# One stage of a chunked RWKV-7 scan is woven in two slots earlier, an addition moves from VectorE to TensorE, and three PSUM results share one bank

## The chip, the cores and the metric

The kernel runs on one core of one Trainium2 chip. The metric is the device time of one execution in microseconds. Names of engines in the profile: PE is TensorE's matrix multiplication, PEld its weight load, DVE is VectorE, ACT is ScalarE, POOL is GpSimd, SP is SyncE, which here only issues DMAs. `L12` is line 12 of the kernel that was profiled.

## The reference

A two-layer encoder over 256 positions of width 2048. Each layer normalises its input, multiplies it by one wide input projection, runs two head groups on the result, gates both, joins them and multiplies by an output projection, which is added to the residual:

```
for l in range(DEPTH):                       # DEPTH = 2
    h = rms_norm(x, norm_g[l])
    proj = h @ w_in[l]
    r, k, v, xw, xa = split(bidir_token_shift(proj[:, :3264]))
    y_rw = rwkv7_branch(r, k, v, xw, xa, ...)     # 16 heads of 64, one scan per direction
    y_at = window_attention(rope(q), rope(k_at), v_at, sink[l])
    x = x + concat([y_rw * silu(g_rw), y_at * silu(g_at)]) @ w_out[l]
return rms_norm(x, final_g)

def step(S, inp):                            # of the RWKV-7 scan, S is 64 x 64 for a head
    s_kk = S @ kk_t
    S = S * w_t - outer(s_kk, a_t * kk_t) + outer(v_t, k_t)
    return S, S @ r_t
```

The kernel replaces the 256 steps by four chunks of 64. Within a chunk the recurrence becomes a triangular system, whose inverse is built by doubling blocks and then corrected by one Newton step; the change touches that correction and the loop over chunks.

## The kernel before, in words

**The stream.** The projections are a list of steps (`Stream`, L222). A step is three matmuls on fp32r tiles (`gemm`, L273 to L275: high part of the weights by high part of the input, high by low, low by high), all 128 by 128 by 256. Eight steps use one tile of weights. It comes by DMA from SP's queue, is rounded to `hi` on ACT (L215) and has the rest put into `lo` on DVE (L216), in two halves each; two tiles have buffers.

**Windows and slots.** Everything else is woven into this stream. `layer` runs the stream 64 steps at a time (`window`, L359), and a window is cut into 14 slots. At the head of each slot some generators are advanced by one `yield`, then four or five stream steps follow. PE executes in exactly this written order (`manual_schedule`). The other engines' orders are made by the scheduler at build time, by priority, and are fixed in the program; each engine runs its own list in order. Two heads are a pair, and pair `p` goes through these generators:

- `scan_p` (L631, window `p + 1`, slots `STAGE_P`): low-rank products for decay and in-context rate (`pza`), their scans along the chunk (`lw`, L659 on DVE), the exponentials `pp` and `ip` on ACT (L662, L663), a sum over each head (`pk`, L628), reciprocal `kd` (L665 on DVE), and the operands `MV` and `BK`.
- `scan_i` (L708, window `p + 2`, every slot, and slots 0 and 1 of window `p + 3`): Gram products `pg` for direction 0 in slot 0 and for direction 1 in slot 1 (L718), both masked on DVE into `ge` (L724); a 16-bit copy `AB` on ACT (L733); in slot 2 transposes into `pt` (L741, L749), which ACT copies out as `bt` (L754) and into `suv` (L759); from slot 3 on the doubling of the inverse, with `pq` and `pd` on PE (L803, L813, L819, L821), `QF` on ACT (L815), `tv` and `tt` on DVE (L806, L822, L823). In slots 0 and 1 of the next window the Newton step: residual `pf` (L829 to L834), its copy `q16` on ACT (L836), product `pn` (L840), and `vf` = 2 `tt` + `pn` on DVE (L842).
- `scan_b` (L848, window `p + 3`, slots 1 to 13, and slot 3 of window `p + 4`): four chunk steps of three slots each. In the first slot PE multiplies the state (`pcc`, L866), ACT copies it to `rh` (L869, L872). In the second PE applies the inverse (`pu`, L885) and ACT writes the result into `suv` (L890). In the third PE updates the state (L895) and the output `py` (L902), and DVE scales the state into `suv` for the next chunk (L897). Slots 12 and 13 make the head norm (L913 to L917). The part in the next window's slot 3 is called the tail here: eight transposing matmuls (L922, 16 records in the trace), ACT's scale and bias (L924), DVE's L925 and L614, ACT's L615, DVE's L616.

So windows 1 to 8 of a layer hold a `scan_p`, 2 to 9 a `scan_i`, 3 to 10 a `scan_b`, 4 to 11 a tail. Window 3 is the one that has all of them except a tail. Windows are counted from 0; in layer 0 window 3 starts at 123.96 us of the trace, window 4 at 166.82 and window 6 at 252.54. Windows from 10 on hold attention.

**PSUM.** The scans share two rotating buffers of two banks each (`wpair`, tag `w`); a new allocation waits until the readers of the one before the last are done. `pcc` and `py` have a bank each. In a window the order of allocation is `pf`, `pg`; `pn`, `pg`; `pu`, `pt`; the tail's `pyt`, `pq`; `pq`, `pza`; and so on. So `pq` in slot 3 takes over the buffer of `pt`, which ACT empties with L754 and L759.

**Quarters of the array.** A matmul with 64 rows and 64 columns uses a quarter of PE's array: the rows are the operands' partition half, the columns the half that the result goes to. `half[h ^ d]` swaps halves for the second direction.

Of the kernel before, what the change touches and what calls it, by code (L numbers as in the profile page):

```python
# [21 lines left out]
T = 256  # L22
# [19 lines left out]


SLOTS = 14
STAGE_P = [4, 6, 7, 8, 9, 10, 11, 13]
STAGE_I = (list(range(SLOTS)), [0, 1])
STAGE_B = (list(range(1, 14)), [3])
ATT = [
    [4, 11],
    [1, 3, 6, 8, 11, 13],  # L50
# [78 lines left out]
def hybrid_trunk_kernel(ctx, tc, xT, wi, wv, wo, par, fing, dup, iup, sink, pos, cst, out):  # L129
# [21 lines left out]
    def wbank(name):  # L151
        return wpair(name)[:, 0]

    def st(tag, shape, dt=F32, bufs=1):
        return sp.tile([128, *shape], dt, tag=tag, name=tag, bufs=bufs)
# [140 lines left out]
    LV = cp.tile([128, NL, 2, 128], U8, name="LV")  # L296
    AB, AL, QF = (cp.tile([128, 2, NC, 64], F16, name=n) for n in ("AB", "AL", "QF"))
    MSK = cp.tile([128, NC, 64], F16, name="MSK")
    EYE, NEYE = (cp.tile([128, 64], F16, name=n) for n in ("EYE", "NEYE"))
    band = cp.tile([128, 512], BF16, name="band")  # L300
    FG = cp.tile([128, NKT], F32, name="FG")
    SK = cp.tile([128, DEPTH * 16], F32, name="SK")
# [3 lines left out]
    def setup():  # L306
        posi = st("t1", [T], I32, bufs=3)
        SY.dma_start(out=posi, in_=pos.to_broadcast([128, T]))
        SY.dma_start(out=FG, in_=fing)
        SY.dma_start(out=SK, in_=sink.to_broadcast([128, DEPTH * 16]))  # L310
        cin = st("mv", [C_N - C_KEEP], bufs=3)
        SY.dma_start(out=cin, in_=cst[:, C_KEEP:C_N])
        for l in range(DEPTH):
            s = DP[:, l, 0:NSH]
            V.tensor_tensor(s, PR[:, l, P_MU0 : P_MU0 + NSH], PR[:, l, P_MU1 : P_MU1 + NSH], op=ALU.add)
            V.tensor_scalar(s, s, -1.0, 1.0, op0=ALU.mult, op1=ALU.add)
            h = DP[:, l, NSH : NSH + 8]
            V.tensor_scalar(h, PR[:, l, P_KA : P_KA + 8], 0.5, None, op0=ALU.mult)
            V.tensor_scalar(DP[:, l, NSH + 8 : NSH + 16], h, -1.0, 1.0, op0=ALU.mult, op1=ALU.add)
            V.tensor_scalar(DP[:, l, NSH + 16 : NSH + 32], PR[:, l, P_A0 : P_A0 + 16], 0.5, None, op0=ALU.mult)  # L320
        V.tensor_scalar(SK, SK, 8.0, None, op0=ALU.mult)
        yield


        ang = st("g", [T], bufs=2)
        nn = st("g", [T], bufs=2)
        V.tensor_copy(ang, posi)
        V.tensor_scalar(ang, ang, C[:, C_OFF["inv"] : C_OFF["inv"] + 1], None, op0=ALU.mult)

        def reduce_by(dst, src, period, bits, shift):  # L330
            V.tensor_scalar(nn, src, 1.0 / period, shift, op0=ALU.mult, op1=ALU.add)
            V.tensor_scalar(nn, nn, MAGIC, MAGIC, op0=ALU.add, op1=ALU.subtract)
            cur = src
            for p in split_const(period, bits, 4):
                V.scalar_tensor_tensor(dst, nn, -p, cur, op0=ALU.mult, op1=ALU.add)
                cur = dst

        two_pi = 2.0 * np.pi
        reduce_by(ang, ang, two_pi * 4096.0, 7, 0.0)
        for dst, shift, add in ((SIN, 0.0, 0.0), (COS, 0.25, np.pi / 2)):  # L340
            reduce_by(dst, ang, two_pi, 11, shift)
            if add:
                V.tensor_scalar(dst, dst, float(add), None, op0=ALU.add)
            V.tensor_scalar(dst, dst, PI_IN, -PI_IN, op0=ALU.min, op1=ALU.max)
            A.activation(dst, dst, AF.Sin)
        V.tensor_scalar(SIN, SIN, C[:, C_OFF["sgn"] : C_OFF["sgn"] + 1], None, op0=ALU.mult)
        yield
        V.tensor_copy(
            LV.rearrange("p l s (n x) -> p (l s) n x", x=32),
            cin[:, 512 : 512 + 64 * NL].rearrange("p (n x) -> p n x", x=32).unsqueeze(2).to_broadcast([128, 2 * NL, NC, 32]),  # L350
        )
        V.memset(MSK, 1.0)
        V.memset(MSK[:, :, 0:1], 0.0)
        V.tensor_copy(band, cin[:, 0:512])
        V.tensor_copy(EYE, cin[:, 512 + 64 * NL : 576 + 64 * NL])
        V.tensor_scalar(NEYE, EYE, -1.0, None, op0=ALU.mult)
        yield

    def window(n, *gens, groups=SLOTS):  # L359
# [246 lines left out]
    def layer(l):  # L606
# [24 lines left out]
        def scan_p(p, t):  # L631
# [18 lines left out]
            KR = st("kkr", [T])  # L650
            A.activation(KR, K, AF.Identity, scale=prm(P_KK, p))
            yield
            pk = wbank("pk")
            head_sums(pk, sq)

            V.tensor_scalar(LW, LW, 1.0, None, op0=ALU.add)
            msk = MSK.rearrange("p c j -> p (c j)")
            for x in (LW[:, 0:T], LW[:, T : 2 * T][:, ::-1]):
                V.tensor_tensor_scan(x, msk, x, 0.0, op0=ALU.mult, op1=ALU.add)  # L659
            PP = st("pp", [2, NC, 64])  # L660
            IP = st("ip", [2, NC, 64])
            A.activation(PP.rearrange("p d c j -> p (d c j)"), LW, AF.Exp, scale=DECAY_C)  # L662
# [45 lines left out]
        def scan_i(p, t):  # L708
# [126 lines left out]
            FN = st("q16", [2, NC, 64], F16)  # L835
            A.activation(FN.rearrange("p d c j -> p d (c j)"), pf[:, :, 0:T], AF.Copy)  # L836
            yield
            pn = wbank("pn")
            for d, c, h in dch:
                PE.matmul(pn[half[h ^ d], d * T + c * 64 : d * T + (c + 1) * 64], hx(FN, d, c, h), hx(TT, d, c, h), start=True, stop=True)  # L840
            VF = st("vf", [2, NC * 64])
            V.scalar_tensor_tensor(  # L842
                VF.rearrange("p d x -> p (d x)"), TT.rearrange("p d c j -> p (d c j)"), 2.0, pn, op0=ALU.mult, op1=ALU.add
            )
            t["VF"] = VF
            yield

        def scan_b(p, t):  # L848
            GE, MV, BT, SUV, PC, bv = (t[n] for n in ("GE", "MV", "BT", "SUV", "PC", "bv"))


            pc = ps_c.tile([128, 512], F32, tag="c", name="pcc")
            pS = pc[:, 0:128].rearrange("p (d j) -> p d j", d=2)
            pyt = ps_c.tile([128, 512], F32, tag="y", name="py")
            py = pyt[:, 0:256].rearrange("p (c j) -> p c j", j=64)
            for i in range(NC):
                ci = [order[d][i] for d in range(2)]

                here = lambda h, i=i: pick(SUV, half[h], i * 128 + h * 64, [NC * 128 + (NC - 1 - 2 * i) * 128, 2], [1, 64])

                pr = [pc[:, 128:192], pc[:, 192:256] if i else pyt[:, 256:320]]
                for d in range(2):
                    for h in range(2):

                        r = half[1 - h] if i == 0 else every
                        PE.matmul(pr[d][half[h ^ d]], GE[h][r, d, ci[d], 0, :], SUV[r, d, ci[d], h, :], start=True, stop=True)  # L866
                RH = st("rh", [2, 64], bufs=2)
                if i:
                    A.activation(RH, pc[:, 128:256].rearrange("p (d j) -> p d j", d=2), AF.Copy)  # L869
                else:  # L870
                    for d in range(2):
                        A.activation(RH[:, d, :], pr[d], AF.Copy)  # L872
                yield
                if i > 0:
                    for d in range(2):
                        for h in range(2):
                            PE.matmul(
                                py[half[h], ci[d], :], MV[half[h], d, ci[d], 1, :], SUV[half[h], d, ci[d], h, :],
                                start=False, stop=False, skip_group_check=True,
                            )  # L880
                pu = wpair("pu")
                for d in range(2):
                    for h in range(2):
                        x = half[h ^ d]
                        PE.matmul(pu[half[h], d, 0:64], t["VF"][x, d, cs(ci[d])], RH[x, d, :], start=True, stop=True)  # L885
                if 0 < i < NC - 1:
                    for h in range(2):
                        PE.matmul(pS[half[h]], ident[half[h], half[h]], here(h), start=True, stop=False, skip_group_check=True)  # L888
                for h in range(2):
                    A.activation(here(h), pu[half[h], :, 0:64], AF.Copy)  # L890
                yield
                if i < NC - 1:
                    for d in range(2):
                        for h in range(2):
                            PE.matmul(pS[half[h], d, :], BT[:, h, d, i, :], SUV[:, d, ci[d], h, :], start=(i == 0), stop=True, skip_group_check=True)  # L895
                    for h in range(2):
                        V.tensor_tensor(  # L897
                            here(h, i + 1), pS[half[h]], pick(PC, half[h], i, [2 * NC - 1 - 2 * i, 2], [0, 64]), op=ALU.mult
                        )
                for d in range(2):  # L900
                    for h in range(2):
                        PE.matmul(  # L902
                            py[half[h], ci[d], :], GE[h][:, d, ci[d], 1, :], SUV[:, d, ci[d], h, :],
                            start=(i == 0 and d == 0), stop=(i >= NC // 2), skip_group_check=True,
                        )
                if i < NC - 1:
                    yield
# [8 lines left out]
            yield  # L916
            V.tensor_tensor(ysq, py, yv.unsqueeze(2).to_broadcast([128, NC, 64]), op=ALU.mult)  # L917
            yield
            pz = wbank("pyt")
            for c in range(NC):  # L920
                for h in range(2):
                    PE.matmul(pz[half[h], cs(c)], ysq[half[h], c, :], ident[half[h], half[h]], start=True, stop=True)  # L922
            Zt = st("t1", [T], bufs=3)
            A.activation(Zt, pz[:, 0:T], AF.Identity, scale=prm(P_LG, p), bias=prm(P_LB, p))  # L924
            V.tensor_tensor(Zt, Zt, bv, op=ALU.add)  # L925
            mix_split(p, Zt, t["gr"])
            yield
# [217 lines left out]
```

## Time and profile before

| | |
|---|---|
| median of three runs | 1244.04 us (1242.3 to 1247.03) |
| the profiled execution | 1247.3 us, of which the span of the trace is 1245.5 us |
| PE busy | 1184.3 us, 95% of the span |
| DVE busy | 937.5 us, 75% |
| ACT busy | 739.9 us, 59% |
| mean granted clock of TensorE | 0.987 |

A row of a timeline reads: start, duration, engine, line, operation, what it writes and reads, its form, how many were merged, and in brackets the idle time of the engine before it and who ended that. In the view of waits a row reads: who waited, for whom, us in total, times, the longest. Slots can be found in the timeline by their PE lines: L840 opens slot 1, L885 with L741 slot 2, L895 with L902 and L803 slot 3, and L895 opens slot 9 as well.

### The profile page before, as it was taken

What the parts mean: (1) busy time and instruction counts of PE and PEld (TensorE: products, weight loads), DVE (VectorE), ACT (ScalarE), POOL (GpSimd) and SP (SyncE); (2) the same over time, 40 slices, a digit from 0 to 9 for tenths busy, and PEclk for the clock granted to TensorE, in tenths of its full rate; (3) what the DMA queues carried; (4) which work ended last, traced back from release to release, by engine and by line L of the source; (5) the groups of instructions that cost most, each with busy time, mean ns of one, the idle gap of its engine ahead of it and who ended that gap; (6) DMA issues with size and microseconds to landing.
All of it is one profiled execution on the core that took longest, in us unless ns stands there. A gap on an engine that the chain in (4) does not pass through costs nothing.

```text
span 1245.5 us, 38032 instructions
## 1 busy us (share of the span) xinstructions
PE 1184.3 (95%) x16140; PEld 1092.3 (88%) x16140; DVE 937.5 (75%) x2082; ACT 739.9 (59%) x1838; POOL 19.0 (2%) x23
## 2 busy tenths in 40 slices
PE   6989999999998999999999999999999989999996
PEld 6978888888887989989998888888888888899996
DVE  6878878887976678856666888878887766786654
ACT  6646665766565466645555656665766555675553
POOL 0000000000000000000000000000000000000000
PEclk9999999999999999999999999999999999999998
DMA  7443233322322434466554433233223324435653
GB/s 246 156 143 122 88 116 109 105 93 94 134 77 93 133 109 142 140 204 224 210 182 143 143 110 119 93 111 109 104 93 100 112 99 131 140 130 174 212 190 119
DMA packets 60410, 166.70 MB, mean 134 GB/s; under 512 B 7728, under 2 KB 22736, under 8 KB 60240
## 3 DMA queue, kind: packets, MB, share of 16 engines
q1 hardware_dynamic: 60240, 164.27, 38.5%
q8 instruction: 126, 2.06, 0.7%
q14 instruction: 44, 0.36, 0.1%
HBM read 157.43 MB, written 4.19 MB: 130 GB/s over the span
## 4 chain that ended last, share of the span: by engine, by line
PE 48%; DVE 18%; issue 16%; ACT 11%; DMA 4%; SPq 1%; POOL 0%; DVEq 0%; POOLq 0%; ACTq 0%
PE pm L273 13%; PE pm L275 11%; PE pm L274 11%; DVE lo L216 3%; DMA g<-dup 3%; PE pg L718 2%; DVE kd L665 2%; ACT hi L215 2%; DVE ge L724 2%; ACT AB L733 2%; ACT suv L759 2%; DVE lw L659 2%; ACT ge L771 1%; DMA rrot<-u 1%; ACT bt L754 1%
## 5 line engine op out<-in xcount | busy, mean ns | idle before, releaser
L273 PE MATMUL pm<-XH,hi 128*128 128x256 f32 x1664 | 498.1, 299 | 14.5 <-ACT XH L178 6.1
L275 PE MATMUL pm<-XH,lo 128*128 128x256 f32 x1664 | 471.4, 283 | 11.2 <-DVE lo L216 11.2
L274 PE MATMUL pm<-XL,hi 128*128 128x256 f32 x1664 | 470.6, 283 | 0.1
L215 ACT ACTIVATE hi<-raw 128x512 fp32r<-128x512 f32 x560 | 329.6, 625 | 212.1 <-PE pm L274 170.0
L216 DVE TENSOR_TENSOR lo<-raw,hi 128x512 fp32r<-128x512 f32 x560 | 369.0, 687 | 84.0 <-ACT hi L215 76.7
L273 PEld LDWEIGHTS pm<-XH,hi 128*128 128x128 f32 x1664 | 316.5, 190 | 40.2 <-issue 13.0
L275 PEld LDWEIGHTS pm<-XH,lo 128*128 128x128 f32 x1664 | 316.8, 190 | 14.6 <-DVE lo L216 14.4
L274 PEld LDWEIGHTS pm<-XL,hi 128*128 128x128 f32 x1664 | 317.3, 191 | 0.8 <-DVE XL L179 0.8
L273 PE MATMUL pm<-MH,hi 128*128 128x256 f32 x512 | 145.5, 284 | 2.3 <-ACT hi L215 2.3
L275 PE MATMUL pm<-MH,lo 128*128 128x256 f32 x512 | 145.2, 284 | 0.1
L274 PE MATMUL pm<-ML,hi 128*128 128x256 f32 x512 | 145.0, 283 | 0.0
L273 PEld LDWEIGHTS pm<-MH,hi 128*128 128x128 f32 x512 | 97.9, 191 | 3.2 <-ACT hi L215 2.5
L275 PEld LDWEIGHTS pm<-MH,lo 128*128 128x128 f32 x512 | 97.8, 191 | 0.4 <-DVE lo L216 0.4
L274 PEld LDWEIGHTS pm<-ML,hi 128*128 128x128 f32 x512 | 98.0, 191 | 0.0
L890 ACT ACTIVATE suv<-pu 64x128 f32<-64x128 f32 x128 | 34.5, 270 | 24.8 <-PE pcc L888 13.6
L724 DVE TENSOR_TENSOR ge<-pg,C 128x1024 f32<-128x1024 f32 x32 | 39.1, 1221 | 3.5 <-PE pg L718 3.5
L970 ACT ACTIVATE mv<-mv,mx 128x257 f32<-128x257 f32 x64 | 31.9, 504 | 15.9 <-DVE mx L967 15.9
L733 ACT ACTIVATE AB<-ge 64x512 f16<-64x512 f32 x32 | 20.2, 630 | 34.3 <-DVE ge L724 33.9
L718 PE MATMUL pg<-mv,bk 64*128 64x128 f32 x512 | 37.2, 285 | 0.0
L822 DVE CAST_PREDICATED tv<-LV,pd 128x256 f16<-128x256 uint8 x80 | 34.0, 426 | 4.1 <-PE pd L821 3.7
L815 ACT ACTIVATE QF<-pq 128x256 f16<-128x256 f32 x80 | 30.8, 385 | 6.8 <-PE pq L813 5.5
L823 DVE CAST_PREDICATED tt<-LV,pd 128x256 f16<-128x256 uint8 x80 | 34.0, 425 | 0.0
(241 smaller groups left out, 1833.7 us busy)
## 6 DMA issues: line engine op xcount, KB each, us to landing
raw<-wi SPq DMA_DIRECT2D x207, 512.0 KB, 3.8
raw<-wo SPq DMA_DIRECT2D x64, 512.0 KB, 3.8
raw<-wv SPq DMA_DIRECT2D x8, 512.0 KB, 3.6
rrot<-u SPq DMA_DIRECT2D x80, 32.0 KB, 2.3
vg<-xT SPq DMA_DIRECT2D x16, 128.0 KB, 3.6
xd<-vg SPq DMA_DIRECT2D x16, 128.0 KB, 3.6
vg<-xd SPq DMA_DIRECT2D x16, 128.0 KB, 3.5
g<-dup SPq DMA_DIRECT2D x16, 97.0 KB
```

The lines of the kernel that those rows point to most:

```text
L215: A.activation(hi[:, q], raw[:, q], AF.Copy)
L216: V.tensor_tensor(lo[:, q], raw[:, q], hi[:, q].bitcast(F32), op=ALU.subtract)
L273: PE.matmul(pm, wh, rh[:, kk, :], start=(kk == 0), stop=False)
L274: PE.matmul(pm, wh, rl[:, kk, :], start=False, stop=False)
L275: PE.matmul(pm, wl, rh[:, kk, :], start=False, stop=(kk == 15))
L718: PE.matmul(pg[:, h, c * 128 : (c + 1) * 128], BK[half[h], d, c, 1 - h : 3 - h, :].rearrange("p s j -> p (s j)"), MV[half[h], d, c].rearra ...
L724: V.tensor_tensor(GEd(d), pg.rearrange("p h (c x) -> p h c x", c=NC), gm[d].unsqueeze(1).unsqueeze(1).to_broadcast([128, 2, NC, 128]), op= ...
L733: A.activation(flat(AB[half[h]]), GE[h][half[h]].rearrange("p d c s j -> p (d c) s j")[:, :, 0, :], AF.Copy)
L822: V.copy_predicated(t_sub(TC), t_mask, flat4(pd[:, :, 0:128]))
L823: V.copy_predicated(v_sub(TT), v_mask, flat4(pd[:, 0, 128:384].rearrange("p (d x) -> p d x", d=2)))
L890: A.activation(here(h), pu[half[h], :, 0:64], AF.Copy)
L970: A.activation(Sc[:, h, q, 0:257], Sc[:, h, q, 0:257], AF.Exp, scale=0.125, bias=mx[:, q : q + 1], accum_out=den[:, q : q + 1])
```

## The change

- `STAGE_P` gets a slot more, and `scan_p` a `yield` more: the decays' scans (L656, L659) are emitted in slot 5, and the head sum `pk` with the rest stays in slot 6.
- `STAGE_B`: the tail moves from slot 3 to slot 1 of the next window, where it stands on PE ahead of the Newton product.
- `vf`: four matmuls by twice the identity (`EYE2`) add 2 `tt` in PSUM, and ACT copies the sum out. DVE's L842 is gone. `pn` gets a buffer of two banks in place of one.
- `rh` and `pu` come out on the partitions of their own head in both directions. L885's four products before used all four quarters of the array; they now all stand on the two diagonal ones. L840's sixteen went the other way, from the diagonal to all four. L866 in the first chunk went from four quarters to the two off the diagonal.
- The state product, the product with the inverse and the state are thirds of one `pcc` tile, made anew in each chunk step; `pu` no longer comes from the rotating buffers, and the tail's result goes into the second half of `py`'s bank. ACT's copy of `rh` in the first chunk is one instruction in place of two.

```diff
-STAGE_P = [4, 6, 7, 8, 9, 10, 11, 13]
+STAGE_P = [4, 5, 6, 7, 8, 9, 10, 11, 13]
-STAGE_B = (list(range(1, 14)), [3])
+STAGE_B = (list(range(1, 14)), [1])
...
-            pk = wbank("pk")
-            head_sums(pk, sq)
             V.tensor_scalar(LW, LW, 1.0, None, op0=ALU.add)
...
                 V.tensor_tensor_scan(x, msk, x, 0.0, op0=ALU.mult, op1=ALU.add)
+            yield
+            pk = wbank("pk")
+            head_sums(pk, sq)
...
-            pn = wbank("pn")
+            pn = wpair("pn")
+            for d in range(2):
+                for h in range(2):
+                    PE.matmul(
+                        pn[half[h], d, 0:T], EYE2[half[h ^ d]], TT[half[h ^ d], d].rearrange("p c j -> p (c j)"), start=True, stop=False, skip_group_check=True
+                    )
             for d, c, h in dch:
-                PE.matmul(pn[half[h ^ d], d * T + c * 64 : d * T + (c + 1) * 64], hx(FN, d, c, h), hx(TT, d, c, h), start=True, stop=True)
+                PE.matmul(pn[half[h], d, cs(c)], hx(FN, d, c, h), hx(TT, d, c, h), start=False, stop=True, skip_group_check=True)
-            V.scalar_tensor_tensor(
-                VF.rearrange("p d x -> p (d x)"), TT.rearrange("p d c j -> p (d c j)"), 2.0, pn, op0=ALU.mult, op1=ALU.add
-            )
+            A.activation(VF, pn[:, :, 0:T], AF.Copy)
...
+                pc = ps_c.tile([128, 3, 2, 64], F32, tag="c", name="pcc")
+                pS = pc[:, 2]
...
-                        PE.matmul(pr[d][half[h ^ d]], GE[h][r, d, ci[d], 0, :], SUV[r, d, ci[d], h, :], start=True, stop=True)
+                        PE.matmul(pc[half[h], 0, d, :], GE[h][r, d, ci[d], 0, :], SUV[r, d, ci[d], h, :], start=True, stop=True)
...
-                pu = wpair("pu")
                 for d in range(2):
                     for h in range(2):
-                        x = half[h ^ d]
-                        PE.matmul(pu[half[h], d, 0:64], t["VF"][x, d, cs(ci[d])], RH[x, d, :], start=True, stop=True)
+                        PE.matmul(pc[half[h], 1, d, :], t["VF"][half[h], d, cs(ci[d])], RH[half[h], d, :], start=True, stop=True)
...
-            pz = wbank("pyt")
+            pz = pyt[:, T : 2 * T]
```

Two places show how the engines' lists move. The first is DVE in slots 0 to 3 of window 6 of layer 0, before. `ge` is the masked Gram product (L724, direction 0 and then 1), `vf` the corrected inverse, the rows with `t` and `mf` belong to the tail:

```order
L784 COPY tv<-EYE 128x512
L724 TENSOR_TENSOR ge<-pg,C 128x2x512
L842 SCALAR_TENSOR_TENSOR vf<-tt,pn 128x512
L784 COPY tt<-EYE 128x512
L724 TENSOR_TENSOR ge<-pg,C 128x2x512
L764 TENSOR_TENSOR AL<-ge,AB 64x512 x2
L808 COPY_PREDICATED tt<-LV,AB 128x128
L216 TENSOR_TENSOR lo<-raw,hi 128x512
L897 TENSOR_TENSOR suv<-pcc,pc 64x2x64 x2
L925 TENSOR_TENSOR t_4588<-t_4588,bv 128x256
L806 COPY_PREDICATED tv<-LV,pq 128x2x128
L614 SCALAR_TENSOR_TENSOR mf<-t_4588,vg 128x256
```

The same place in the changed kernel; its line numbers are its own, L726 being `ge`, and L923, L615 and L617 the tail's three:

```order
L786 COPY tv<-EYE 128x512
L726 TENSOR_TENSOR ge<-pg,C 128x2x512
L923 TENSOR_TENSOR t_4475<-t_4475,bv 128x256
L786 COPY tt<-EYE 128x512
L615 SCALAR_TENSOR_TENSOR mf<-t_4475,vg 128x256
L617 TENSOR_TENSOR ML<-mf,MH 128x256
L726 TENSOR_TENSOR ge<-pg,C 128x2x512
L766 TENSOR_TENSOR AL<-ge,AB 64x512 x2
L810 COPY_PREDICATED tt<-LV,AB 128x128
L216 TENSOR_TENSOR lo<-raw,hi 128x512
L895 TENSOR_TENSOR suv<-pcc,pc 64x2x64 x2
L808 COPY_PREDICATED tv<-LV,pq 128x2x128
```

The tail's three DVE instructions now stand between the two `ge`, and `vf` is gone from this list.

The second place is ACT in slots 4 to 6 of the same window, before. `suv` is the copy that the state update in slot 6 reads, `pp` the exponential of the decays:

```order
L869 ACTIVATE rh<-pcc 128x128
L400 ACTIVATE kr<-u,DP 128x256
L815 ACTIVATE QF<-pq 128x2x64x2
L441 ACTIVATE duh<-g 97x256
L441 ACTIVATE iuh<-g 96x256
L644 ACTIVATE lw<-pza 128x512
L647 ACTIVATE th<-pza,DP 128x256 x2
L890 ACTIVATE suv<-pu 64x2x64 x2
L662 ACTIVATE pp<-lw 128x512
L663 ACTIVATE ip<-lw 128x512
```

And in the changed kernel, where `suv` is L888 and `pp` L664:

```order
L401 ACTIVATE kr<-u,DP 128x256
L872 ACTIVATE rh<-pcc 128x128
L817 ACTIVATE QF<-pq 128x2x64x2
L442 ACTIVATE duh<-g 97x256
L442 ACTIVATE iuh<-g 96x256
L645 ACTIVATE lw<-pza 128x512
L648 ACTIVATE th<-pza,DP 128x256 x2
L664 ACTIVATE pp<-lw 128x512
L888 ACTIVATE suv<-pcc 64x2x64 x2
L665 ACTIVATE ip<-lw 128x512
```

`pp` now stands ahead of `suv`. Window 3 has this second order already before the change, and from slot 3 to slot 10 the lists of DVE and ACT in the changed kernel's windows 4 to 7 are those of window 3 before.

More of the change, by code (lines that the diff above doesn't have):

```diff
@@ L298, in hybrid_trunk_kernel @@
     MSK = cp.tile([128, NC, 64], F16, name="MSK")
-    EYE, NEYE = (cp.tile([128, 64], F16, name=n) for n in ("EYE", "NEYE"))
+    EYE, NEYE, EYE2 = (cp.tile([128, 64], F16, name=n) for n in ("EYE", "NEYE", "EYE2"))
     band = cp.tile([128, 512], BF16, name="band")
@@ L356, in setup @@
         V.tensor_scalar(NEYE, EYE, -1.0, None, op0=ALU.mult)
+        V.tensor_scalar(EYE2, EYE, 2.0, None, op0=ALU.mult)
         yield
@@ L849, in scan_b @@
             GE, MV, BT, SUV, PC, bv = (t[n] for n in ("GE", "MV", "BT", "SUV", "PC", "bv"))
-            pc = ps_c.tile([128, 512], F32, tag="c", name="pcc")
-            pS = pc[:, 0:128].rearrange("p (d j) -> p d j", d=2)
             pyt = ps_c.tile([128, 512], F32, tag="y", name="py")
@@ L859, in scan_b @@
                 here = lambda h, i=i: pick(SUV, half[h], i * 128 + h * 64, [NC * 128 + (NC - 1 - 2 * i) * 128, 2], [1, 64])
-                pr = [pc[:, 128:192], pc[:, 192:256] if i else pyt[:, 256:320]]
+                pc = ps_c.tile([128, 3, 2, 64], F32, tag="c", name="pcc")
+                pS = pc[:, 2]
                 for d in range(2):
@@ L865, in scan_b @@
                         r = half[1 - h] if i == 0 else every
-                        PE.matmul(pr[d][half[h ^ d]], GE[h][r, d, ci[d], 0, :], SUV[r, d, ci[d], h, :], start=True, stop=True)
+                        PE.matmul(pc[half[h], 0, d, :], GE[h][r, d, ci[d], 0, :], SUV[r, d, ci[d], h, :], start=True, stop=True)
                 RH = st("rh", [2, 64], bufs=2)
[L868 to L872, printed above, removed]
+                A.activation(RH, pc[:, 0], AF.Copy)
                 yield
@@ L889, in scan_b @@
                 for h in range(2):
-                    A.activation(here(h), pu[half[h], :, 0:64], AF.Copy)
+                    A.activation(here(h), pc[half[h], 1], AF.Copy)
                 yield
@@ L923, in scan_b @@
             Zt = st("t1", [T], bufs=3)
-            A.activation(Zt, pz[:, 0:T], AF.Identity, scale=prm(P_LG, p), bias=prm(P_LB, p))
+            A.activation(Zt, pz, AF.Identity, scale=prm(P_LG, p), bias=prm(P_LB, p))
             V.tensor_tensor(Zt, Zt, bv, op=ALU.add)
```

## Prediction

> **What bounds the kernel now.** The page's busy times come first, then the view of waits.
>
> ```profile
> span 1245.5 us, 38032 instructions
> PE 1184.3 (95%) x16140; PEld 1092.3 (88%) x16140; DVE 937.5 (75%) x2082; ACT 739.9 (59%) x1838; POOL 19.0 (2%) x23
> ...
> PE pq L803 <- ACT suv L759: 11.6, 12, 1.5
> PE pm L275 <- DVE lo L216: 11.2, 15, 1.6
> PE pm L273 <- ACT hi L215: 6.2, 4, 2.3
> PE pt L741 <- DVE ge L724: 3.0, 2, 1.7
> ```
>
> PE is the bound, with few waits. The largest is the one that the new PSUM layout aims at: `pq` in slot 3 takes over the buffer that ACT empties with L759. It occurs 12 times, 11.6 us in all. After the change `pu` and the tail's `pyt` no longer stand in that rotation, `pq` gets the buffer of a `pg` that has long been read, and this wait goes.
>
> What that is worth I read from two windows of layer 0. Window 6 has every generator. Window 3 has all but a tail, so its rotation is one allocation shorter and its `pq` does not wait: a trial of the new layout inside the old kernel. PE's timeline, window 3 and then 6, each from slot 1 to the next slot 1:
>
> ```profile
> 127.19 0.34 PE L840 MATMUL pn<-tt,q 64*64 64x64 f16 x10
> ...
> 133.39 0.45 PE L895 MATMUL pcc<-suv,bt 128*64 128x64 f32 x8
> 134.01 0.33 PE L803 MATMUL pq<-tv,AB 64*64 64x32 f16 x10
> ...
> 150.55 0.30 PE L813 MATMUL pq<-tv,AB 64*64 64x32 f16 x16 [0.26 <-DVE tt L823]
> 153.21 0.39 PE L275 MATMUL pm<-XH,lo 128*128 128x256 f32 x1 [0.48 <-DVE lo L216]
> 153.52 0.45 PE L895 MATMUL pcc<-suv,bt 128*64 128x64 f32 x8
> 170.02 0.34 PE L840 MATMUL pn<-tt,q 64*64 64x64 f16 x10
> ```
>
> ```profile
> 255.74 0.34 PE L840 MATMUL pn<-tt,q 64*64 64x64 f16 x10
> 261.95 0.68 PE L922 MATMUL pyt<-C,ysq 64*64 64x64 f32 x16
> 262.56 0.45 PE L895 MATMUL pcc<-suv,bt 128*64 128x64 f32 x8
> 264.11 0.33 PE L803 MATMUL pq<-tv,AB 64*64 64x32 f16 x11 [0.86 <-ACT suv L759]
> 282.07 0.45 PE L895 MATMUL pcc<-suv,bt 128*64 128x64 f32 x8
> 298.58 0.34 PE L840 MATMUL pn<-tt,q 64*64 64x64 f16 x10
> ```
>
> Slot 1 to slot 1 takes 298.58 - 255.74 = 42.84 us in window 6 and 170.02 - 127.19 = 42.83 us in window 3. Up to slot 9 both take 26.33 us (282.07 - 255.74, 153.52 - 127.19). From L895 to L803 window 6 spends 1.55 us and window 3 0.62, so 0.93 less, and window 3 has no L922 either, 0.61 us (261.95 to 262.56). Yet it isn't shorter: 1.54 us come back further on, 0.26 and 0.48 of it as marked waits and the rest in the slots with `suv` and `lo`. So in window 3 something besides PE sets the pace. ACT's and DVE's timelines there show a chain:
>
> ```profile
> 128.91 1.23 DVE L724 TENSOR_TENSOR ge<-pg,C 128x1024 f32<-128x1024 f32 x1 [0.22 <-PE pg L718]
> 136.74 0.69 DVE L216 TENSOR_TENSOR lo<-raw,hi 128x512 fp32r<-128x512 f32 x1 [1.58 <-ACT hi L215]
> 140.91 1.27 DVE L659 TENSOR_TENSOR_SCAN lw<-MSK,lw 128x256 f32<-128x256 f16 x2
> 152.46 1.29 DVE L216 TENSOR_TENSOR lo<-raw,hi 128x512 fp32r<-128x512 f32 x2
> ```
>
> ```profile
> 130.16 1.28 ACT L733 ACTIVATE AB<-ge 64x512 f16<-64x512 f32 x2 [2.10 <-DVE ge L724]
> 136.07 1.68 ACT L215 ACTIVATE hi<-raw 128x512 fp32r<-128x512 f32 x3
> 142.22 0.63 ACT L662 ACTIVATE pp<-lw 128x512 f32<-128x512 f32 x1 [1.52 <-DVE lw L659]
> 142.76 0.55 ACT L890 ACTIVATE suv<-pu 64x128 f32<-64x128 f32 x2
> ```
>
> The mask of direction 1 (L724, 128.91) ends at 130.14 and ACT's `AB` starts 0.02 later. ACT then works through its list to `hi` at 136.07, for which DVE stood idle 1.58 us. DVE goes on to the scans (140.91), `pp` on ACT waited 1.52 us for these, and `suv`, which PE needs for the state in slot 6, stands behind `pp`. DVE's `lo` at 152.46 closes it, 0.48 us late. In the changed kernel the lists of ACT and DVE in slots 3 to 10 of windows 4 to 7 read as those of window 3 do here, with the scans ahead and `pp` in front of `suv`. So this chain is what takes over when the wait at L803 goes, and what matters is when its head, the mask, starts.
>
> **The change part by part.**
>
> *The tail in slot 1.* Its instructions now stand between the two masks on DVE. DVE runs its list in order, so the mask of direction 1 waits for the whole tail: PE, ACT, DVE, ACT, DVE in turn. The rows of window 6:
>
> ```profile
> 264.63 0.57 ACT L924 ACTIVATE t<-pyt,PR 128x256 f32<-128x256 f32 x1
> 266.54 0.41 ACT L615 ACTIVATE MH<-mf 128x256 fp32r<-128x256 f32 x1
> ```
>
> ```profile
> 256.23 0.69 DVE L842 SCALAR_TENSOR_TENSOR vf<-tt,pn 128x512 f32<-128x512 f16 x1
> 256.95 0.29 DVE L784 COPY tt<-EYE 128x512 f16<-128x512 f16 x1
> 257.46 1.23 DVE L724 TENSOR_TENSOR ge<-pg,C 128x1024 f32<-128x1024 f32 x1 [0.22 <-PE pg L718]
> ...
> 265.23 0.42 DVE L925 TENSOR_TENSOR t<-t,bv 128x256 f32<-128x256 f32 x1 [1.58 <-ACT t L924]
> 266.04 0.41 DVE L614 SCALAR_TENSOR_TENSOR mf<-t,vg 128x256 f32<-128x256 f32 x1
> 267.50 0.41 DVE L616 TENSOR_TENSOR ML<-mf,MH 128x256 fp32r<-128x256 f32 x1
> ```
>
> L922 0.68 + L924 0.57 + L925 0.42 + L784 0.29 + L614 0.41 + L615 0.41 + L616 0.41 = 3.19 us from the start of slot 1 to the mask. Now it is 257.46 - 255.74 = 1.72. **The mask starts 1.47 us later.** All of it is on the chain, and behind it on DVE's list stand `tt`, `lo` and the state's scaling; `AB`, `bt` and `suv` wait on ACT. That PE also spends 0.61 us on L922 ahead of L718 is inside these 1.47, as is L842's absence. In slot 3 the tail costs nothing any more, but window 3 shows that its absence there gains nothing while the chain sets the pace. Bounds: 0.65 if the mask need not wait for the tail (rival B), 1.8 with wake-up time of 0.05 us at each of six handovers.
>
> *L885 on diagonal quarters.* The nearest rows of one shape, sixteen records each, are these two, on four quarters and on two:
>
> ```profile
> 259.47 0.41 PE L741 MATMUL pt<-C,vg 64*64 64x64 f32 x16
> ```
>
> It takes 0.41 us against L922's 0.68, so sixteen records lose 0.27 and the eight of L885 about 0.13 (estimate). Four groups a window; those in slots 2, 5 and 8 lie in time that the chain leaves to PE, and only that in slot 11 counts: +0.13. Bounds 0 and 4 x 0.13 = 0.52. L840 from two quarters to four and L866 from four to two roughly cancel; I take 0.
>
> *2 `tt` on TensorE.* Four matmuls of 64 by 256 in 16 bit, which stand ahead of L840 on PE; the residual's four of that kind take 0.13 us, from one start to the next:
>
> ```profile
> 252.54 0.30 PE L829 MATMUL pf<-tv,NEYE 64*64 64x256 f16 x4
> 252.67 0.20 PE L833 MATMUL pf<-tv,AB 64*64 64x64 f16 x4
> ```
>
> They need only `tt`, which was there before. If they were to come ahead of the tail they would add 0.13 to the mask; they come behind it, so they don't. DVE's 16 x 0.69 = 11.0 us go; L842 ended before the mask could start (0.22 us idle), so this is no time of the span. ACT gets a copy of the same size in its idle 2.1 us. `rh` in one instruction: nothing.
>
> *The scans a slot ahead.* They stand ahead of the two products behind them, as in window 3. `pp` is then in front of `suv` on ACT, which is how the chain reaches PE in slot 6. Already in the 26.33 us.
>
> *The sum.* Windows 4 to 7 of two layers: 8 x (1.47 + 0.13) = +12.8. Window 3: 2 x (0.13 for L885 + 0.13 for the four matmuls, which have no tail ahead of them) = +0.5. Window 8 has no key mixing in its lists, and I take 0. In window 9 the waits of L741 (3.0 in two) and two of L803 at about 1.5 go, 6.0 in all; in their place come the later mask, 2 x 1.47, and the rest of the new chain, 0.2 each (estimate): -2.6, between -6.0 and +3. Window 10, where the tail stands among attention: 0 to +1 each, 0.5 taken, +1.0. **Together +11.7 us on the span of 1245.5, so 1257.2.** The profiled execution took 1247.3 us, 1.8 over its span and 3.3 over the median of 1244.0. On the median: 1244.0 + 11.7 = 1255.7 us.
>
> **The rivals.** About 0.5%, 6.2 us, is what a measurement of this kernel can tell from no change: faster is below 1237.8, slower above 1250.3.
>
> *B, the mask comes late by PE alone.* If ACT and DVE do the tail faster than its rows add up, the mask waits only for L718 behind L922: +0.65 and 0.13, 8 x 0.78 = 6.2, with the other terms (0.5 - 2.6 + 1.0) +5.1: 1249.1 us. Against it stands the written order of DVE's list.
>
> *C, the other side: faster.* If PE sets the pace and window 3's chain is slow for reasons of its own, a window gets 0.93 of the wait and 0.61 of L922 in slot 3 back and pays 0.65 in slot 1 and 0.52 for L885: -0.37, eight times -3.0, with -0.7 for window 8, +1.3 for window 3 at PE's price, -2.6 and +1.0: -4.0, 1240.0 us. It decides if the chain from mask to slot 9 is at least 0.5 us shorter than in window 3, with the tail's work out of slots 3 to 5. For it speaks only that window 6 shows no wait of PE behind L803. Against it, the tail's work isn't in window 3 either. With the mask held less and PE's other waits of 17 us for `lo` and `hi` shorter too it reaches 1235.
>
> *D, the clock.* Rows of windows (stretch, us, busy of five engines, granted clock, DMA share, GB/s):
>
> ```profile
> 252.00:295.00 43.00, 41.99 (x754) 37.83 (x753) 36.02 (x77) 27.84 (x73) 1.01 (x1) 1.00 0.32 104
> 555.00:562.00 7.00, 6.53 (x29) 6.23 (x30) 4.36 (x10) 3.46 (x8) 0.00 (x0) 0.51 0.62 203
> ```
>
> The clock stayed at 1.00 in window 6 with its wait of 0.86 us, and was 0.51 in a stretch that follows the longest wait of PE, 2.3 us. The new waits are spread over slots 2, 6 and 9. Should two of them fall together, PE runs at half speed for some 3.5 us: 1.7 us lost a window, 13.6 more, 1269.3 us. The Trainium skill, "TensorE: Matmul & The Clock Gate", Part 1, says that the gate goes cold only after an idle window of about 3.4 us. By that rule none of these waits could do it and D would be worth nothing; the trace's drop after 2.3 us speaks for a shorter limit. I leave D in.
>
> *That the change doesn't do what it says* is half true in A already: the wait at L803 goes and PE waits in slots 6 and 9 instead.
>
> **How the numbers follow.** A, the forecast, 0.57 (1252 to 1261 by the widest bounds, those of window 9; 0.04 of it is kept for less than 1250.3, should half of the hold in slot 1 be absorbed); B 0.14, two thirds of it within 0.5%; C 0.22, half of it within 0.5% and half faster; D 0.07. Slower: 0.53 + 0.04 + 0.07 = 0.64; same: 0.04 + 0.10 + 0.11 = 0.25; faster 0.11. The range from 1238 to 1261 leaves out D and the faster half of C. A's own range is 1252 to 1261.
>
> **What would show it.** In windows 4 to 7 of the profile after: L803's counterpart without a wait; the mask of direction 1 about 3.2 us behind slot 1, idle for ACT's or DVE's tail ahead of it; waits of PE in slot 6 for `suv` and in 8 or 9 for `lo`; a window of 44.4 us. A period of 42.5 would mean C, 43.6 B. A clock under 0.95 in a window would mean D. The forecast is wrong if the mask is late and the window is not: then the chain had slack.

## The result: 0.7% slower, and the profile after

| | before | after |
|---|---|---|
| median of six runs each | 1245.87 us | 1254.57 us (1251.45 to 1256.8) |
| ratio | | 1.0071, 95% interval 1.0051 to 1.0091 |
| profiled execution, and its span | 1247.3, 1245.5 us | 1253.19, 1251.3 us |
| window 6, slot 1 to slot 1 | 42.84 us | 44.28 us |

The head of the page and the view of waits of the changed kernel:

```profile
span 1251.3 us, 38155 instructions
PE 1186.6 (95%) x16204; PEld 1094.6 (87%) x16204; DVE 928.8 (74%) x2067; ACT 747.3 (60%) x1838; POOL 19.0 (2%) x23
...
PE pm L275 <- DVE lo L216: 20.3, 27, 1.6
PE pcc L893 <- ACT suv L888: 10.0, 11, 1.7
```

The 11.6 us of `pq` behind ACT's copies, at the head of this list before, are gone from it. In their place `lo` has 20.3 us, where it had 11.2, and PE's state product L893 waits 10.0 us for `suv`. PE is busy 2.3 us longer, the span 5.8. In window 6 alone, before and then after (stretch, length, busy time of PE, PEld, DVE, ACT and POOL, granted clock, DMA share, GB/s):

```profile
255.74:298.58 42.84, 41.83 (x752) 37.66 (x751) 35.88 (x76) 27.84 (x73) 1.01 (x1) 1.00 0.31 105
```

```profile
256.26:300.54 44.28, 42.50 (x756) 38.28 (x755) 35.48 (x75) 28.34 (x73) 1.01 (x1) 1.00 0.31 102
```

Of the 1.44 us by which the window is longer, 0.67 are more busy time of PE, and 0.77 are more time in which it stands idle. Line numbers here are the changed kernel's: L920 is the tail's transposition, L726 the mask, L658 the scan, L664 `pp`, L888 `suv`, L893 the state product that opens slots 3, 6 and 9.

PE in window 6, from slot 1 to the next slot 1 at 300.54:

```profile
256.26 0.56 PE L920 MATMUL py<-C,ysq 64*64 64x64 f32 x12
263.11 0.45 PE L893 MATMUL pcc<-suv,bt 128*64 128x64 f32 x8
263.72 0.33 PE L805 MATMUL pq<-tv,AB 64*64 64x32 f16 x10
273.79 0.45 PE L893 MATMUL pcc<-suv,bt 128*64 128x64 f32 x8 [0.84 <-ACT suv L888]
283.62 0.39 PE L275 MATMUL pm<-XH,lo 128*128 128x256 f32 x1 [0.81 <-DVE lo L216]
283.94 0.45 PE L893 MATMUL pcc<-suv,bt 128*64 128x64 f32 x8
```

L805, the first `pq`, has no bracket any more: it doesn't wait. PE waits in slot 6 for `suv` and at the end of slot 8 for `lo`. DVE in the same window shows where that begins:

```profile
255.46 1.22 DVE L726 TENSOR_TENSOR ge<-pg,C 128x1024 f32<-128x1024 f32 x1
257.59 0.43 DVE L923 TENSOR_TENSOR t<-t,bv 128x256 f32<-128x256 f32 x1 [0.92 <-ACT t L922]
257.93 0.28 DVE L786 COPY tt<-EYE 128x512 f16<-128x512 f16 x1
258.13 0.42 DVE L615 SCALAR_TENSOR_TENSOR mf<-t,vg 128x256 f32<-128x256 f32 x1
259.03 0.42 DVE L617 TENSOR_TENSOR ML<-mf,MH 128x256 fp32r<-128x256 f32 x1 [0.48 <-ACT MH L616]
259.37 1.22 DVE L726 TENSOR_TENSOR ge<-pg,C 128x1024 f32<-128x1024 f32 x1
...
267.17 0.69 DVE L216 TENSOR_TENSOR lo<-raw,hi 128x512 fp32r<-128x512 f32 x1 [1.73 <-ACT hi L215]
271.35 1.27 DVE L658 TENSOR_TENSOR_SCAN lw<-MSK,lw 128x256 f32<-128x256 f16 x2
```

```profile
260.62 1.28 ACT L735 ACTIVATE AB<-ge 64x512 f16<-64x512 f32 x2 [1.62 <-DVE ge L726]
272.66 0.63 ACT L664 ACTIVATE pp<-lw 128x512 f32<-128x512 f32 x1 [1.53 <-DVE lw L658]
273.20 0.54 ACT L888 ACTIVATE suv<-pcc 64x128 f32<-64x128 f32 x2
```

DVE stands idle twice inside the tail, 0.92 and 0.48 us, each time for ACT, while the second mask stands behind the tail in its list. This delay is called the hold below. That mask starts at 259.37, 3.11 us behind slot 1 (1.72 before). From mask to `suv` it is 13.83 us (273.20 - 259.37); in window 3 of the kernel before it was 13.85 (142.76 - 128.91). From mask to slot 9 it is 24.57, and was 24.61.

### The profile page after: what moved, and what is told of

It is laid out like the page before. It is cut to its first block, busy times and chain, and to the rows that moved or that the text cites. A ratio compares the mean times of both kernels' runs of the same rounds, so it can differ in the third digit from the quotient of the medians.

```text
span 1251.3 us, 38155 instructions
## 1 busy us (share of the span) xinstructions
PE 1186.6 (95%) x16204; PEld 1094.6 (87%) x16204; DVE 928.8 (74%) x2067; ACT 747.3 (60%) x1838; POOL 19.0 (2%) x23
## 5 line engine op out<-in xcount | busy, mean ns | idle before, releaser
L273 PE MATMUL pm<-XH,hi 128*128 128x256 f32 x1664 | 495.9, 298 | 13.9 <-ACT XH L178 6.4
L273 PEld LDWEIGHTS pm<-XH,hi 128*128 128x128 f32 x1664 | 314.5, 189 | 40.0 <-issue 13.0
L273 PE MATMUL pm<-MH,hi 128*128 128x256 f32 x512 | 144.8, 283 | 1.6 <-ACT hi L215 1.6
L273 PEld LDWEIGHTS pm<-MH,hi 128*128 128x128 f32 x512 | 97.4, 190 | 2.6 <-ACT hi L215 1.8
L888 ACT ACTIVATE suv<-pcc 64x128 f32<-64x128 f32 x128 | 34.4, 269 | 16.2 <-PE pq L815 10.9
L726 DVE TENSOR_TENSOR ge<-pg,C 128x1024 f32<-128x1024 f32 x32 | 39.0, 1218 | 3.0 <-PE pg L720 3.0
```

The source lines that it names most:

```text
L273: PE.matmul(pm, wh, rh[:, kk, :], start=(kk == 0), stop=False)
L726: V.tensor_tensor(GEd(d), pg.rearrange("p h (c x) -> p h c x", c=NC), gm[d].unsqueeze(1).unsqueeze(1).to_broadcast([128, 2, NC, 128]), op= ...
L888: A.activation(here(h), pc[half[h], 1], AF.Copy)
```

## The experiments

Eight kernels were run, in two groups. Their times are compared with 20 and 22 runs of the kernel before on the same chips, medians 1244.97 and 1244.98 us.

| run | window 6, slot 1 to slot 1 | median, us | ratio to before (95%) |
|---|---|---|---|
| late_tail | 43.34 | 1249.88 | 1.0039 (1.0021 to 1.0057) |
| tail_slot3 | 45.13 | 1285.42 | 1.0358 (1.0288 to 1.0428) |
| tail_alone | 43.41 | 1251.12 | 1.0046 (1.0031 to 1.0061) |
| scan_p_later | 42.70 | 1234.81 | 0.9917 (0.9888 to 0.9946) |
| old_scan_later | 43.70 | 1251.14 | 1.0049 (1.0033 to 1.0065) |
| late_scan_later | 42.33 | 1238.61 | 0.9951 (0.9932 to 0.9970) |
| tail_alone_scan_later | 43.13 | 1249.40 | 1.0028 (1.0013 to 1.0044) |
| tail_late_scan_later | 43.59 | 1250.42 | 1.0054 (1.0033 to 1.0075) |

**The tail behind the masks (late_tail).** Is it the hold of the mask that costs?

```diff
-for lag, scan, at in ((4, scan_b, STAGE_B[1]), (3, scan_i, STAGE_I[1]), (3, scan_b, STAGE_B[0]), (2, scan_i, STAGE_I[0]), (1, scan_p, STAGE_P)):
+for lag, scan, at in ((3, scan_i, STAGE_I[1]), (2, scan_i, STAGE_I[0]), (4, scan_b, STAGE_B[1]), (3, scan_b, STAGE_B[0]), (1, scan_p, STAGE_P)):
```

> The changed kernel with the tail of slot 1 written behind the Newton product and both Gram masks instead of ahead of them; everything else as in the change. Theory A (the tail holds the mask of direction 1, and the chain from mask to slot 9 passes that on): the mask starts about 1.85 us after slot 1 instead of 3.11 (1.72 before, and 0.13 for the four products by twice the identity), of which 0.41 us is lost again because ACT's third step of the tail now stands between the two copies AB. A window of 43.4 us (up to 44.0, as ip now also stands ahead of suv) instead of 44.28, 5 to 7 us less in all. Rival (the hold is harmless, the other parts of the change cost the time): 44.3 us a window, no change against the changed kernel.

Its mask on DVE's timeline, in a window whose slot 1 starts at 254.75:

```profile
256.43 1.23 DVE L726 TENSOR_TENSOR ge<-pg,C 128x1024 f32<-128x1024 f32 x1 [0.90 <-PE pg L720]
```

It starts 1.68 us behind slot 1 and waits for PE alone. The window is 43.34 us, as theory A had it: 0.94 less than in the changed kernel, of the 1.44 us that a window had become longer. That is the net effect of the edit: it also moves the tail's later steps on ACT and DVE, and `ip` now stands ahead of `suv` too. Over before, the kernel is 4.9 us slower where the changed one was 8.7, so 3.8 less, a little under the 5 to 7 expected.

**The tail back in slot 3 (tail_slot3).**

```diff
-STAGE_B = (list(range(1, 14)), [1])
+STAGE_B = (list(range(1, 14)), [3])
```

> The changed kernel with the tail back in slot 3, the rest of the change kept. The mask is free (1.85 us after slot 1), but the tail's pieces on ACT and DVE stand on the same chain in slots 3 and 4, ahead of the roundings hi and lo, and exp (pp) still stands ahead of suv on ACT. Theory A, by the chain: 1.26 us less for the mask, 0.57 of ACT and 0.34 + 0.34 + 0.2 of DVE more behind it: 44.4 us a window, 43.9 at the least, so no gain to speak of against the changed kernel. Rival (only the place of the tail in slot 1 costs): 42.8 to 43.0 us a window as before the change, 11 us less.

Both were wrong: 45.13 us a window, and 40 us more than before in all. PE in slot 3:

```profile
266.26 0.45 PE L893 MATMUL pcc<-suv,bt 128*64 128x64 f32 x8
268.84 0.45 PE L900 MATMUL py<-suv,ge 128*64 128x64 f32 x8 [2.12 <-ACT t L922]
```

The tail's result now lies in the bank of `py`. In slot 3 the next pair's `py` (L900) needs that bank and waits 2.12 us for ACT to have read the tail. The eight windows 4 to 7 are 23 us longer in all than before, and windows 8 and 9, where L900 waits up to 4.1 us, 18. In three of the eight the clock fell to half for 3.4 us (one of them from 223.71 on). So in the new layout the tail must come earlier: the move and the shared bank are one edit. The run doesn't tell what the tail in slot 3 would cost with a bank of its own.

**The tail alone (tail_alone).** The kernel before, with nothing but the tail's new slot.

```diff
-STAGE_B = (list(range(1, 14)), [3])
+STAGE_B = (list(range(1, 14)), [1])
```

> The kernel before with one edit: the tail in slot 1 instead of slot 3. Nothing of PSUM's layout, quarters, TensorE sum or scans is changed. Theory A: pq in slot 3 gets pu's buffer by the rotation, so the wait behind ACT's copies goes without the new layout, and the same hold comes: L922 0.61, pn 0.4, vf 0.69 and the tail's 0.42 + 0.29 + 0.41 + 0.41 + 0.41 put the mask 3.6 us behind slot 1; 44.7 us a window (44.3 to 45.4), 12 to 20 us slower than before. Rival (layout, quarters or the sum on TensorE cost the time): 42.8 us a window, no change against before.

PE in window 6:

```profile
255.63 0.68 PE L922 MATMUL pyt<-C,ysq 64*64 64x64 f32 x16
256.98 1.16 PE L718 MATMUL pg<-mv,bk 64*128 64x128 f32 x16 [0.27 <-ACT t L924]
263.41 0.33 PE L803 MATMUL pq<-tv,AB 64*64 64x32 f16 x10
```

L803 has no wait, without the new layout: with the tail allocated in slot 1 the rotation gives `pq` the buffer of `pu`. The mask starts at 259.00, 3.37 us behind slot 1, so the hold is there. The window grew by 0.57 us and not by 1.9, and the kernel by 6 us and not by 12 to 20. DVE's list shows most of the difference:

```profile
260.38 0.69 DVE L216 TENSOR_TENSOR lo<-raw,hi 128x512 fp32r<-128x512 f32 x1 [0.16 <-ACT hi L215]
...
266.69 1.29 DVE L216 TENSOR_TENSOR lo<-raw,hi 128x512 fp32r<-128x512 f32 x2 [1.10 <-ACT hi L215]
267.90 0.48 DVE L401 SCALAR_TENSOR_TENSOR kr<-u,PR,kr 128x255 f32<-128x255 f32 x1
```

One of the three `lo` of slots 4 and 5 stands right behind the mask here, and the evacuation L399 ahead of the other two. From the first `lo` of the group to `kr` it is 1.21 us (267.90 - 266.69), in the changed kernel 2.15 (L402 there at 269.32, `lo` at 267.17): 0.94 us of the chain had moved into an idle place. With the mask 0.2 us earlier than the 3.6 expected, that is 1.2 of the 1.3 us missing. A sum that carries the mask's delay to the end holds only while the list behind it stays the same.

**scan_p one slot later (scan_p_later).** The other end of the chain.

```diff
-STAGE_P = [4, 5, 6, 7, 8, 9, 10, 11, 13]
+STAGE_P = [5, 6, 7, 8, 9, 10, 11, 12, 13]
```

> The changed kernel with scan_p one slot later (stages 5 to 13 instead of 4 to 13), so that suv stands ahead of pp on ACT as it did before the change; the tail stays in slot 1 and holds the mask. Theory A (the chain reaches PE through suv behind pp and through the roundings behind the scans): the mask stays at 3.1 us, but PE's wait of 0.84 us in slot 6 goes and that of 0.81 in slot 9 goes or shrinks: 42.6 to 43.4 us a window. Rival (DVE's own work from the mask to slot 9 sets the pace, whatever its order): 44.3 us.

```profile
252.50 0.56 PE L920 MATMUL py<-C,ysq 64*64 64x64 f32 x12
```

```profile
255.61 1.22 DVE L726 TENSOR_TENSOR ge<-pg,C 128x1024 f32<-128x1024 f32 x1
```

```profile
266.05 0.56 ACT L888 ACTIVATE suv<-pcc 64x128 f32<-64x128 f32 x2 [0.49 <-PE pcc L886]
...
270.76 0.63 ACT L664 ACTIVATE pp<-lw 128x512 f32<-128x512 f32 x1
```

The mask is held exactly as long as in the changed kernel, 3.11 us (255.61 - 252.50). But `suv` is written 4.7 us ahead of `pp`, not behind it, and PE shows no wait in windows 4 to 7. A window is 42.70 us, 1.58 less than with the change and 0.14 less than before it. So the hold costs little by itself; it costs through the chain, and the chain reaches PE where `suv` and `lo` stand behind scan_p's work.

Window 6, from slot 1 to the next:

```profile
252.50:295.20 42.70, 42.48 (x756) 38.30 (x755) 35.30 (x75) 28.54 (x73) 1.01 (x1) 1.00 0.33 106
```

PE is as busy as in the changed kernel, 0.65 us more than before (41.83), so little of the wait that went is left over. The kernel is 0.8% or 10 us faster than the one before, of which windows 4 to 7 give only 8 x 0.14 = 1.1 us. Window 3 takes 41.71 us in both layers, where before took 42.83 and 42.84; window 8 takes 42.4 us, where before, with waits of 2.9 and 2.6 us, took 44.8 and 44.4; window 9 takes 41.9 and 41.2, where before took 43.4 (with half clock in it) and 42.2. The clock had a part too: its mean has a median of 0.993 in the five runs, and of 0.990 in the 20 of before. How the rest divides between them was not taken apart.

**Without the change (old_scan_later)**: the kernel before, `STAGE_P = [5, 7, 8, 9, 10, 11, 12, 13]`.

> The kernel before with scan_p one slot later (stages 5, 7 to 13) and nothing of the change: the tail in slot 3, the old PSUM layout. Theory A: the wait of pq behind ACT's copies (0.82 to 0.86 us a window) is set by the head of ACT's list, which doesn't move, and PE sets the pace behind it; 42.8 us a window as before, within 4 us of before in all. Rival (the later scan_p is worth the time by itself, and the run with it was fast without help from the change): 41.9 to 42.1 us a window, 6 us or more less than before.

Neither: 43.70 us, 0.86 more than before, and the view of waits shows what is late.

```profile
PE pq L803 <- ACT suv L759: 11.5, 12, 1.5
...
PE pq L813 <- ACT suv L890: 6.5, 10, 0.6
...
PE pza L622 <- ACT suv L890: 3.4, 12, 0.3
```

The old wait stays as theory A had it, and two new ones come: `pq` in slot 8 and `pza` in slot 5 take over a buffer of `pu`, which ACT empties with L890. That is again PSUM's rotation, in other slots. The later scan_p pays only with `pu` out of it.

**The hold taken away as well (late_scan_later)**: the edits of late_tail and scan_p_later together.

> The changed kernel with scan_p one slot later and the tail behind both masks: the hold of the mask goes from a kernel in which the chain no longer reaches PE. Theory A (the hold costs only through that chain): no gain against scan_p one slot later alone, 42.6 to 42.8 us a window there as here. Rival (the hold costs by itself): 1.2 us a window less, 41.4 to 41.6.

Slot 1 to slot 1 took 42.3 to 42.6 us in windows 4 to 7, 0.1 to 0.4 less than with scan_p_later, not 1.2: theory A in the main. In all it is no faster, 1238.61 us, 0.5% less than before where scan_p_later has 0.8%. Its four waits of L893 for `suv`, 6.5 us, lie outside windows 4 to 7.

**The old layout, tail moved, scan_p later (tail_alone_scan_later)**: the diffs of tail_alone and old_scan_later together.

> The kernel before with two edits: the tail in slot 1 and scan_p one slot later; old PSUM layout, L885 on four quarters, sum on VectorE. Theory A: the rotation alone gives pq the buffer of pu, so the wait goes, and the chain stays off PE. PE's own work without that wait is 42.84 - 0.86 = 41.98 us, plus 0.27 for the wait of L718 behind the tail's scale that the tail alone showed: 42.1 to 42.5 us a window, 0.2 to 0.6 less than scan_p_later's 42.70, because L885 keeps four quarters and no products by twice the identity are added; 3 to 5 us less than that run in all and 10 to 16 less than before. Rival (PSUM's new layout is what makes it fast): 42.8 us or more.

The rival was right: 43.13 us a window, 0.43 more than with the changed layout (scan_p_later).

```profile
PE pq L813 <- ACT suv L890: 6.5, 10, 0.6
...
PE pza L622 <- ACT suv L890: 3.4, 12, 0.3
PE pg L718 <- ACT t L924: 3.2, 12, 0.3
```

The same two waits on `pu`'s buffer, and the one on the tail's. The new layout is worth its products on two quarters and its sum on TensorE once scan_p is moved.

**The same with the tail behind the masks (tail_late_scan_later).**

> As the run before, but with the tail written behind both masks. Theory A: L718 no longer waits for the tail's scale and the mask is free; PE alone: 42.0 to 42.3 us a window, as fast as the run before or 1 to 2 us faster in all. Rival (ACT's and DVE's third and fourth step of the tail between the copies AB push suv onto PE's path): 42.6 or more.

43.6 us a window, in the rival's range, but not by its mechanism: the largest new waits of PE don't name `suv`.

```profile
PE pza L622 <- DVE tt L823: 6.8, 12, 0.7
PE pu L885 <- DVE kd L665: 5.8, 10, 0.6
```

L622 writes `pza` and L885 `pu`, both from the old rotation. They wait for `tt`, a reader of `pd`, and for `kd`, the reader of `pk`. Theory A's sum from PE's own work failed here as in the run before, by waits for PSUM buffers. That the rotation is the cause is read from who waits for whom; no run took it away here.

## Why the prediction was right, point by point

- **The wait at L803 goes.** Right. But the new layout, to which the prediction put it down, isn't needed for that: in tail_alone the move of the tail does it alone.
- **What takes its place.** Right: the chain of window 3, from mask to `suv` 13.83 us (13.85 there) and to slot 9 24.57 (24.61). The waits stand in slots 6 and 8 as forecast.
- **The mask.** 3.19 us behind slot 1 was forecast, 3.11 came: 1.39 later than before and not 1.47. The rows of the old tail carried over to its new place. Rival B, PE alone, is out: DVE waits inside the tail for ACT. Late_tail gives 0.94 us a window back, net of what else it moves.
- **L885.** 0.13 us in slot 11 was forecast. From slot 9 to the next slot 1 it is 16.60 us now (283.94 to 300.54), and was 16.51: 0.09, which holds every other difference of these slots too. By the prediction's rows, four groups of L885 and the four products by twice the identity make 4 x 0.13 + 0.13 = 0.65 us more work of PE a window, and its busy time grew by 0.67. That fits but doesn't prove it: tail_alone, with the old layout, has 42.25 us of it (41.83 before). L885 on four quarters within the shared bank was not tried.
- **A window.** +1.60 forecast, +1.44 measured; 11.5 us over eight, where the sum had 12.8.
- **Window 3, 8 and 9.** Window 3 grew by 0.16 us (0.26 forecast). Window 8 became 0.7 and 0.5 us shorter (0 forecast). Window 9 became 0.5 and 0.3 us shorter instead of 1.3 each: L893 there waits up to 1.7 us for `suv`. In layer 0 part of the 0.5 is the clock, which before was at half for 3.4 us in this window.
- **The sum.** From slot 1 of window 3 of layer 1 to the end, neither trace has half clock but in its last 10 to 11 us. Before takes 508.24 us for this (1245.52 - 737.28), after 514.86 (1251.32 - 736.46): +6.6 us, where the prediction had 11.7 / 2 = 5.85 for a layer. Windows 4 to 7 give +5.8 (6.4 forecast), 3 +0.16 (0.26), 8 -0.46 (0), 9 -0.29 (-1.3), and from 10 on +1.45 (0.5). The main term was sized well; that the sum comes so close is partly luck, as the gain in window 9 was put too high and the loss from window 10 on too low, while windows 4 to 8 went the other way.
- **The scans a slot ahead.** The prediction took `pp` in front of `suv` as a consequence of this part. It isn't. Without this part the changed kernel has the same instructions in the same order on every engine. Tail_alone has `pp` in front of `suv` by the tail's move alone, and tail_slot3 has it by the rest of the change without that move, so either is enough. Why the scheduler then chooses this order stays open.
- **The clock.** The medians differ by 8.7 us, not by 11.7. The sum left out a gain. These are stretches of before and then of after, with the granted clock behind the five engines:

```profile
29.00:33.00 4.00, 3.10 (x14) 3.10 (x15) 3.46 (x10) 2.75 (x7) 0.00 (x0) 0.57 0.27 109
398.00:402.00 4.00, 4.00 (x41) 3.62 (x41) 3.52 (x8) 3.07 (x8) 0.00 (x0) 0.57 0.15 47
681.00:685.00 4.00, 3.45 (x16) 3.16 (x17) 3.89 (x8) 3.62 (x10) 0.00 (x0) 0.57 0.00 0
```

```profile
29.00:33.00 4.00, 3.78 (x32) 3.78 (x33) 3.82 (x11) 3.02 (x7) 0.00 (x0) 1.00 0.16 65
398.00:402.00 4.00, 3.96 (x72) 3.63 (x67) 1.86 (x6) 3.89 (x9) 0.00 (x0) 1.00 0.00 0
558.00:562.00 4.00, 4.00 (x23) 4.00 (x23) 2.08 (x5) 1.15 (x3) 0.00 (x0) 0.57 0.72 220
681.00:685.00 4.00, 2.62 (x22) 2.40 (x20) 4.00 (x7) 3.62 (x11) 0.00 (x0) 1.00 0.14 47
```

A mean of 0.57 over 4 us is 3.4 us at half clock. Before had three such stretches and 6.9 us more around 555 (0.51 over 7 us), after only the one at 558: 13.7 us less at half clock, by estimate up to 6.9 us of PE's time. The profiled spans differ by 5.8 us, so without the clock by up to 12.7. Over all runs the mean clock has a median of 0.994 in the six of after (0.993 to 0.995) and of 0.990 in the 42 of before beside the experiments (0.986 to 0.994). A mean lower by 0.004 is about 10 us more at half clock (2 x 0.004 x 1250), by estimate up to 5 us of time, which is enough for the 3 us by which the forecast was too high. Two of the stretches, at 29 and 681 us, lie outside the windows that the change touches; why the changed kernel escapes them is not settled.
- **Rivals C and D.** C said that the chain of window 3 has slack. It has none as the change leaves it. In scan_p_later, with `suv` ahead of `pp`, it no longer reaches PE; a window is then 0.14 us shorter than before where C had 0.37. The gain in all, 10 us, is larger than C's 4 for reasons that C didn't have: windows 3 and 8 of both layers give 2.2 and 4.5 us (C had a loss of 1.3 and a gain of 0.7), and the clock a part. D, a clock that drops in every window, did not come: the clock is 1.00 there. A wait of 2.12 us in tail_slot3 did bring such drops, in three of eight windows. The prediction calls 2.3 us the longest wait of PE; its view of waits leaves out a longer one, of 6.1 us for `XH` (L273), at the start of the program:

```profile
PE pm L273 <- ACT XH L178: 6.1, 1, 6.1
```

It bears on nothing in windows 4 to 7.

## What to carry to other kernels

A wait for a rotating buffer may hide a chain that is just as long: look for a window without the wait, and see whether it is shorter. A step moved ahead of another in one engine's list holds everything behind it for as long as its own partners on other engines take: the hold is the sum of the whole relay, not the busy time there. What the hold costs depends on the list behind it, from 0.94 us a window here to 0.1 to 0.4 with another order. Before such a change is dropped, look at what closes the chain: here one slot of another generator turned 0.7% slower into 0.8% faster, and the same slot without the change cost 0.5%.

## What the runs showed of the hardware

The clock's drops go with PE's share of a stretch of 3.4 us, not with the length of one wait. PE's busy time (first figure after the length) in such a stretch just ahead of a drop, two of the kernel before and one of tail_slot3; then, of the changed kernel, two that no drop followed:

```profile
26.11:29.52 3.41, 1.43 (x10) 1.22 (x10) 1.62 (x5) 0.69 (x2) 0.00 (x0) 1.00 0.98 356
394.75:398.16 3.41, 1.87 (x50) 1.71 (x45) 1.27 (x3) 3.29 (x8) 0.00 (x0) 1.00 0.02 5
```

```profile
220.30:223.71 3.41, 1.41 (x31) 1.29 (x32) 1.89 (x6) 3.21 (x8) 0.00 (x0) 1.00 0.02 5
```

```profile
25.77:29.18 3.41, 1.97 (x15) 1.56 (x13) 2.13 (x6) 0.69 (x2) 0.36 (x1) 1.00 0.99 372
394.41:397.82 3.41, 1.74 (x20) 1.54 (x21) 2.65 (x5) 2.10 (x5) 0.00 (x0) 1.00 0.00 0
```

Here a drop followed on stretches with up to 1.87 of 3.41 us busy, and from 1.74 up there are stretches without one. In every trace the clock changes on a grid of 3.413 us (29.52 and 398.16 in the kernel before are 108 such steps apart). On that grid the ten traces have 3542 stretches at full clock. A drop followed on all 50 with less than 1.68 us busy, on 9 of the 16 between 1.68 and 1.93, and on one of the 3476 with more (late_scan_later at 1224.42, near the end of the program). So the limit lies near half, and the stretch need not be idle. A wait of 1.72 us that two stretches share (it ends at 391.85 in the kernel before) brought no drop: they were busy for 2.2 and 2.9 us. What a drop costs shows in tail_slot3: window 5, with 3.4 us at half clock, took 46.55 us and window 6, without, 45.13, so 1.4 us. The Trainium skill, "TensorE: Matmul & The Clock Gate", Part 1, has the clock fall after an idle window of about 3.4 us. The length agrees; the stretches above that a drop followed were busy for 41 to 55% of it.
